# Input projections by seven block products, values first, with the recurrence done in place

## Chip, cores and metric

The kernel runs on one core of a Trainium2 chip. The metric is device time in microseconds, the median of the runs. The core has a matrix engine (TensorE, PE in the profile, with its weight loads as PEld), VectorE (DVE), ScalarE (ACT), GpSimd (POOL) and SyncE (SP), and queues of DMAs that SP and POOL feed.

## What is computed

A decoder trunk of two layers on 1024 tokens of width 1024. The change lies in the first layer's token mixer, a gated linear recurrence with 8 heads of 128:

```python
proj = h @ w_in                                   # (1024, 4 * 1024)
q, fz, v, g = jnp.split(proj, 4, axis=-1)
q = jax.nn.silu(q)
f = lb + (1 - lb) * jax.nn.sigmoid(fz)
k = 1 - f                                         # log_f = log(max(f, 1e-6))
# per head: S_t = diag(f_t) S_{t-1} + k_t v_t^T,  o_t = S_t^T q_t
o = o * rsqrt(mean(o * o over the head) + 1e-6) * norm_g
out = (o * jax.nn.silu(g)) @ w_out
```

After it come a normalisation with the residual and an MLP (squared ReLU, 4096 wide), then a second layer with a convolution module and an MLP. Those are the same in both kernels.

## The kernel before

**Numbers and products.** Every float32 operand is cut into a high part (ScalarE's copy to a narrower form) and a low part (VectorE's subtraction). A block product is three matmuls per block of the contraction: high by high, high by low, low by high (`product`, L303). Tokens are treated in two halves of 512. A wide matmul is one instruction of 128x512.

**Projections.** `x0T` holds the cut, transposed input, both halves. For each head, q and f (`narrow`, L326) are 8 contraction blocks by 3 matmuls for each half: 768 wide matmuls over all heads, called `ps<-x0T,wa`. Values (`values`, L588) and output gates (`gates`, L432) are computed by token blocks (`wide`, L330): 384 each. Together 1536. The weights come in through `Slots` (L57), which loads by SP, cuts, and keeps a few slots ahead.

**The MLPs already use seven products.** Both MLPs split their matrices into 2x2 blocks and use seven block products in place of eight (`ORDER`, L43: the forms 1, 2, 6, 5, 7, 3, 4); sums of the blocks are needed as operands. For the down weights those sums are made in DRAM by `block_sums` (L402): SP writes one word from a tile that must be ready first (L407), then issues two copies of 1 MB (L408, L409); POOL issues an accumulating DMA of 1 MB (L410) and two of 512 KB (L412), each waiting for the one before it. Fourteen such sums are issued by recurrences 0 to 11, two by each of the first two; the word comes from the recurrence's output tile `o`.

**Recurrence.** `recurrence` (L475) runs 16 times, for 8 heads and 2 halves; I number these 0 to 15. It builds decay products by doubling: at each level n, F and G hold running products from the left and from the right, and `qn`, `kn` (double-buffered) are q and k weighted for that level. Matmuls of `kn` by `qn` give blocks of the score matrix, which a predicated copy with a mask (`put`) brings into A. The levels are 4 (`kd`, `qd`, with reciprocals), 8, 16, 32, 64. Then k is transposed, A and the carried state are multiplied with the values, the state is stepped four times on VectorE, and `o` is stored to DRAM (L581, L582). The heads' norm and gate come later, in `gates`, after reading the heads back; there POOL does the power (L387) of a small tile `ss`.

**Order.** Python emits the work interleaved; a scheduler then fixes one order per engine, and every engine takes its own queue in that order. PSUM has eight banks; the recurrence uses banks 3 to 7 by name (`rps`). The output projection follows the last gates, then the first normalisation.

Of the kernel before, what the change touches and what calls it, by code (L numbers as in the profile page):

```python
# [15 lines left out]
P = 128  # L16
# [220 lines left out]
def body(ctx, tc, d, out):  # L237
# [103 lines left out]
    xraw, rraw = raws(run(128, 4, 4) + run(80, 4, 4)), raws(run(200, 5, 4))  # L341
    wa = Slots(nc, vector, slots(run(96, 4, 8), "wa"), rraw)
    x0T = [half_x(0, "x0T"), half_x(32, "x0T")]

    def load_x(h):
        xt = x0T[h]
        for k in range(0, KB, 2):
            raw = xraw().rearrange("p (a b) -> p a b", a=2)
            nc.sync.dma_start(out=raw, in_=d["xT"][h, :, k : k + 2, :])
            for i in range(2):  # L350
                nc.scalar.copy(out=xt[:, 0, k + i, :], in_=raw[:, i])  # L351
                vector.tensor_tensor(out=xt[:, 1, k + i, :], in0=raw[:, i], in1=xt[:, 0, k + i, :].bitcast(F32), op=ALU.subtract)
            yield xt

    for h in range(H):
        wa.plan([d["wqf"][h, 0], d["wqf"][h, 1]])

    wq, wf, x0 = wa.load(2), wa.load(2), load_x(0)
    for it in (wq, x0, wf, x0, wq, wf, x0, x0):
        next(it)  # L360
    wide_t, rows = (HT,), (NTB, P)
    wv = Slots(nc, vector, slots(run(160, 4, 8), "wv"), rraw)
    wv.plan([d["wv"][n, i] for n in range(2) for i in range(4)] + [d["wg"][0, i] for i in range(4)])
    wv.ahead(4)
    nc.sync.dma_start(out=par, in_=d["par"])
    for _ in load_x(1):
        pass
    vs = ring((64, 80), (2 * NTB, HT), "v")
    p2 = Room(((208, 212),), {"sg": (wide_t, 1), "sq2": (wide_t, 1)})
    p1 = Room(  # L370
        ((128, 160), (192, 200), (212, KBYTES)),
        {
            "mask": ((3, P), 1), "qn": (wide_t, 2), "kn": (wide_t, 2), "at": (rows, 2), "sq": (wide_t, 1), "q": (wide_t, 2), "k": (wide_t, 2),
            "F": (wide_t, 2), "G": (wide_t, 2), "qd": (wide_t, 2), "kd": (wide_t, 2), "dec": ((NTB,), 2), "kt": (rows, 2), "o": (rows, 1), "state": ((P,), 2),
        },
    )
    p1.rings.update(p2.rings)
    rraw = raws(run(200, 2, 4))
    wa.raws = wv.raws = rraw
# [3 lines left out]
    one = cst.tile([P, 1], F32, name="one")  # L383
    nc.gpsimd.memset(one, 1.0)
# [3 lines left out]


    lg = par[:, LB : LB + H]  # L390
    sm = cst.tile([P, 4, H], F32, name="sm")
    lb, oml = cst.tile([P, H], F32, name="lb"), cst.tile([P, H], F32, name="oml")
# [5 lines left out]
    vector.tensor_scalar(out=oml, in0=lb, scalar1=-1.0, scalar2=1.0, op0=ALU.mult, op1=ALU.add)  # L398

# [21 lines left out]


    od = [[dram.tile([P, NTB, HT], F32, name=f"od{n}{h}") for h in range(2)] for n in range(2)]
    yn = [[None, None], [None, None]]

    def heads_back(n):
        for half in range(2):
            yn[n][half] = view(64 + 16 * n + 8 * half, (NTB, HT), F32, "yn")
            nc.sync.dma_start(out=yn[n][half], in_=od[n][half])

    def gates(n, half, t, ws):

        if True:
            ps = acc()
            product(ps, wide(x0T[half], t, ws))
            ov = yn[n][half][:, t, :]
            sg = p2("sg")
            nc.scalar.activation(sg, ps, AF.Sigmoid)
            vector.tensor_tensor(out=sg, in0=ps, in1=sg, op=ALU.mult)
            sq = p2("sq2")  # L440
            nc.scalar.activation(sq, ov, AF.Square)
            ss = stat.tile([P, 2, 4], F32, tag="ss", name="ss")
            vector.tensor_reduce(out=ss[:, 0], in_=sq.rearrange("p (a b) -> p a b", a=4), op=ALU.add, axis=mybir.AxisListType.X)
            nc.gpsimd.tensor_scalar(out=ss[:, 1], in0=ss[:, 0], scalar1=1.0 / P, scalar2=RMS_EPS, op0=ALU.mult, op1=ALU.add)
            power_m_half(ss[:, 0], ss[:, 1], 4)
            for j in range(4):
                oj = ov[:, j * P : (j + 1) * P]
                vector.scalar_tensor_tensor(
                    out=oj, in0=oj, scalar=ss[:, 0, j : j + 1], in1=sg[:, j * P : (j + 1) * P], op0=ALU.mult, op1=ALU.mult
                )  # L450
# [6 lines left out]
    mask = p1("mask")  # L457
    nc.sync.dma_start(out=mask, in_=d["mask"])
    qn, kn, at = ([p1(n) for _ in range(2)] for n in ("qn", "kn", "at"))
    for t in qn + kn + at:  # L460
        nc.gpsimd.memset(t, 0.0)
    count = {"nk": 0, "at": 0}
    vts, carry = {}, {}

    def lr(t, n):
        v = t.rearrange("p (b h n) -> p b h n", h=2, n=n)
        return v[:, :, 0, :], v[:, :, 1, :]

    def last(v, n):
        return v[:, :, n - 1 : n].to_broadcast([P, v.shape[1], n])  # L470
# [4 lines left out]
    def recurrence(h, half, zq, zf, carry):  # L475
        sq = p1("sq")
        nc.scalar.activation(sq, zq, AF.Sigmoid)
        q = p1("q")
        vector.scalar_tensor_tensor(out=q, in0=zq, scalar=QSCALE, in1=sq, op0=ALU.mult, op1=ALU.mult)
        k = p1("k")  # L480
        nc.scalar.activation(k, zf, AF.Sigmoid)
        nc.scalar.activation(k, k, AF.Identity, bias=lb[:, h : h + 1], scale=oml[:, h : h + 1])
        yield
        vt, state = vts[h // 4][0], carry[h]
        F = p1("F")
        vector.tensor_scalar(out=F, in0=k, scalar1=GATE_EPS, scalar2=None, op0=ALU.max)
        nc.scalar.activation(k, k, AF.Identity, bias=one, scale=-1.0)

        G = p1("G")
        (f_l, f_r), (g_l, g_r) = lr(F, 1), lr(G, 1)  # L490
        nc.scalar.copy(out=g_l, in_=f_r)
        nc.vector.memset(g_r, 1.0)
        mul(f_r, f_r, f_l)
# [6 lines left out]
        double(2)  # L500

        (f_l, f_r), (g_l, g_r) = lr(F, 4), lr(G, 4)
        qd = p1("qd")
        kd = p1("kd")
        (q_l, q_r), (k_l, k_r) = lr(q, 4), lr(k, 4)
        vector.reciprocal(lr(qd, 4)[0], g_l)
        mul(lr(qd, 4)[0], q_l, lr(qd, 4)[0])
        mul(lr(qd, 4)[1], q_r, f_r)
        mul(lr(kd, 4)[0], k_l, g_l)
        vector.reciprocal(lr(kd, 4)[1], f_r)  # L510
        mul(lr(kd, 4)[1], k_r, lr(kd, 4)[1])
        A = at[count["at"] % 2]
        count["at"] += 1
        pd = ps1("pd")
        for c in range(NTB):
            tensor.matmul(pd[:, c, :], kd[:, c * P : (c + 1) * P], qd[:, c * P : (c + 1) * P], start=True, stop=True)
# [3 lines left out]

        put(0, pd)
        double(4)
        pc = None
        for n in (8, 16, 32, 64):
            i = count["nk"] % 2
            count["nk"] += 1
            mul(lr(qn[i], n)[1], lr(q, n)[1], lr(F, n)[1])
            mul(lr(kn[i], n)[0], lr(k, n)[0], lr(G, n)[0])
            if n == 8:
                pe = ps1("pe")  # L530
            elif n == 16:
                pc = ps1("pc")
            for c in range(NTB):
                if n <= 16:
                    tensor.matmul(
                        (pe if n == 8 else pc)[:, c, :], kn[i][:, c * P : (c + 1) * P], qn[i][:, c * P : (c + 1) * P], start=True, stop=True
                    )
                else:
                    for s in range(0, P, 2 * n):
                        tensor.matmul(  # L540
                            pc[s : s + n, c, s + n : s + 2 * n],
                            kn[i][:, c * P + s : c * P + s + n],
                            qn[i][:, c * P + s + n : c * P + s + 2 * n],
                            start=True,
                            stop=True,
                        )
            if n == 8:
                put(1, pe)
            double(n)
        put(2, pc)  # L550

        mul(q, q, F)
        mul(k[:, : (NTB - half) * P], k[:, : (NTB - half) * P], G[:, : (NTB - half) * P])
        dec = p1("dec")
        nc.scalar.copy(out=dec, in_=F.rearrange("p (c n) -> p c n", n=P)[:, :, P - 1])
        pk = ps1("pd")
        nk = NTB - half
        for c in range(nk):
            tensor.transpose(pk[:, c, :], k[:, c * P : (c + 1) * P], ident)
        kt = p1("kt")  # L560
        nc.scalar.copy(out=kt[:, :nk], in_=pk[:, :nk])
        po = ps1("po")
        for c in range(NTB):
# [754 lines left out]
```

## Time and profile before

| what | value |
|---|---|
| median of 3 runs | 2153.34 us (2152.73 to 2157.03) |
| span of the profiled execution | 2158.7 us; the page gives no other time for it |
| TensorE busy | 2132.6 us |
| VectorE, ScalarE, POOL busy | 1452.6, 959.1, 374.9 us |
| mean granted TensorE clock | 0.997 |
| first wide matmul | at 6.5 us |
| end of the output projection and its transposes | at 584.3 us |

The page lists groups of instructions by line, engine and operation: busy time, mean duration, and the idle time of that engine ahead of them with what ended it. Other views list waits, instructions in order of time, and busy time by stretches. Idle time on an engine that isn't the bound costs nothing. Helpers record many operations under one line (L172), so the names of tiles tell them apart.

### The profile page before, as it was taken

How to read it: one execution, taken by the hardware profiler on the slowest of the kernel's cores; microseconds unless marked ns; L12 is line 12 of the kernel's file. 1: busy time of each engine (PE TensorE's matmuls, PEld its weight loads, DVE VectorE, ACT ScalarE, POOL GpSimd, SP SyncE). 2: the span in 40 equal slices, each digit the busy share in tenths (PEclk: the TensorE clock that was granted, in tenths of full speed). 3: DMA queues.
4: the chain of work that ended last, by engine and by line, in shares of the span. 5: the costliest groups of instructions: out<-in, count | busy, mean ns of one | idle time of the engine just before them, and what ended most of it. 6: DMA issues, size and time to landing. Idle time of an engine off the chain costs nothing.

```text
span 2158.7 us, 27277 instructions
## 1 busy us (share of the span) xinstructions
PE 2132.6 (99%) x10248; PEld 1772.1 (82%) x10248; DVE 1452.6 (67%) x2107; ACT 959.1 (44%) x1349; POOL 374.9 (17%) x365
## 2 busy tenths in 40 slices
PE   8999999999999999999999999999999999999998
PEld 7888788888888888888888888888878888888887
DVE  7478799867777666556666798899627443554446
ACT  4222232232155555544444576567543443433333
POOL 0011121021100000000001599189211000000001
PEclk9999999999999999999999999999999999999999
DMA  4598888931247776899998855565595988865652
GB/s 182 154 235 227 199 236 214 228 128 59 79 128 272 276 252 227 291 382 322 347 328 313 304 185 186 205 244 174 172 314 189 335 318 310 307 201 194 195 164 99
DMA packets 161349, 494.99 MB, mean 229 GB/s; under 512 B 15040, under 2 KB 43968, under 8 KB 159680
## 3 DMA queue, kind: packets, MB, share of 16 engines
q1 hardware_dynamic: 152256, 459.69, 60.6%
q0 software_dynamic: 8960, 33.56, 8.8%
q8 instruction: 80, 1.31, 0.2%
q14 instruction: 53, 0.43, 0.1%
HBM read 370.50 MB, written 189.79 MB: 260 GB/s over the span
## 4 chain that ended last, share of the span: by engine, by line
PE 86%; DMA 7%; POOL 3%; DVE 2%; ACT 1%; issue 1%; SPq 0%; DVEq 0%; POOLq 0%
PE ps L172 86%; POOL cb L172 2%; DMA y<-kept 1%; DMA raw<-in_w_dram 1%; DMA wa<-ready 1%; DMA raw<-in_wv_dram 1%; DMA dh<-hf 1%; DMA raw<-in_wg_dram 1%; DVE wa L172 0%; DMA raw<-in_wqf_dram 0%; DVE y L172 0%; ACT prod L1086 0%; DMA raw<-in_xT_dram 0%; ACT wa L69 0%; ACT wv L69 0%
## 5 line engine op out<-in xcount | busy, mean ns | idle before, releaser
L172 PE MATMUL ps<-dw,dh 128*128 128x512 f32 x2688 | 611.2, 389 | 0.2 <-ACT dh L69 0.2
L172 PEld LDWEIGHTS ps<-dw,dh 128*128 128x128 f32 x2688 | 504.1, 188 | 104.9 <-ACT dh L69 0.6
L172 PE MATMUL ps<-x1f,fw 128*128 128x512 f32 x1344 | 307.9, 390 | 1.2 <-ACT fw L69 0.8
L172 PEld LDWEIGHTS ps<-x1f,fw 128*128 128x128 f32 x1344 | 251.4, 188 | 53.7 <-ACT fw L69 1.2
L172 PE MATMUL ps<-xa,wa 128*128 128x512 f32 x1152 | 268.8, 392 | 0.0
L172 PEld LDWEIGHTS ps<-xa,wa 128*128 128x128 f32 x1152 | 214.3, 188 | 43.5
L172 POOL TENSOR_TENSOR cb<-cb,prod 128x512 f32<-128x512 f32 x176 | 234.6, 1342 | 17.5 <-ACT prod L1086 7.0
L172 DVE TENSOR_TENSOR dh<-dh 128x1024 fp32r<-128x1024 f32 x112 | 136.3, 1222 | 117.4 <-ACT dh L69 117.2
L172 DVE TENSOR_TENSOR dw<-dr,dw 128x1024 fp32r<-128x1024 f32 x112 | 136.6, 1222 | 103.0 <-ACT dw L69 102.5
L172 DVE SCALAR_TENSOR_TENSOR ps<-u,par,ps 128x512 f32<-128x512 f32 x288 | 198.6, 749 | 9.9 <-ACT ps L1098 8.5
L172 PE MATMUL ps<-x0T,wa 128*128 128x512 f32 x768 | 190.6, 400 | 6.5 <-ACT x0T L351 6.5
L69 ACT CAST dh<-dh 128x1024 fp32r<-128x1024 f32 x112 | 117.0, 1051 | 149.2 <-DMA dh<-hf 148.9
L69 ACT CAST dw<-dr 128x1024 fp32r<-128x1024 f32 x112 | 117.4, 1053 | 134.1 <-PE ps L172 127.8
L172 PE MATMUL ps<-xc,wa 128*128 128x512 f32 x768 | 174.4, 389 | 0.0
L172 PEld LDWEIGHTS ps<-x0T,wa 128*128 128x128 f32 x768 | 143.7, 191 | 35.7 <-ACT x0T L351 6.5
L172 PEld LDWEIGHTS ps<-xc,wa 128*128 128x128 f32 x768 | 144.1, 188 | 29.8
L387 POOL TENSOR_TENSOR mv<-mv,nhalf 128x1 f32<-128x1 f32 x32 | 46.3, 1449 | 687.7 <-DVE mv L172 687.7
L69 ACT CAST wa<-raw 128x1024 fp32r<-128x1024 f32 (+1 forms) x77 | 79.0, 1028 | 192.8 <-PE ps L172 164.7
L172 DVE TENSOR_TENSOR wa<-raw,wa 128x1024 fp32r<-128x1024 f32 (+1 forms) x77 | 95.9, 1248 | 83.4 <-ACT wa L69 83.2
L1086 ACT ACTIVATE prod<-u,par 128x512 f32<-128x512 f32 x176 | 125.3, 722 | 54.4 <-POOL cb L172 53.7
L172 PE MATMUL ps<-wv,x0T 128*128 128x512 f32 x576 | 141.3, 395 | 1.1 <-DVE wv L172 0.8
L172 PEld LDWEIGHTS ps<-wv,x0T 128*128 128x128 f32 x576 | 106.1, 188 | 23.2 <-DVE wv L172 1.1
(177 smaller groups left out, 2606.9 us busy)
## 6 DMA issues: line engine op xcount, KB each, us to landing
wa<-ready SPq DMA_DIRECT2D x122, 512.0 KB, 5.0
dh<-hf SPq DMA_DIRECT2D x112, 512.0 KB, 4.4
ready<-spare SPq DMA_DIRECT2D x74, 512.0 KB, 4.6
sum_w<-in_w_dram SPq DMA_DIRECT2D x32, 1024.0 KB, 9.1
dr<-sum_w SPq DMA_DIRECT2D x64, 512.0 KB, 6.1
raw<-in_w_dram SPq DMA_DIRECT2D x51, 512.0 KB, 3.6
dr<-in_w_dram SPq DMA_DIRECT2D x48, 512.0 KB, 5.5
raw<-in_w1q_dram SPq DMA_DIRECT2D x36, 512.0 KB, 4.4
```

What stands on the lines that cost most here:

```text
L69: self.nc.scalar.copy(out=slot[:, 0, c], in_=raw[:, c])
L172: return op(*args, **kw)
L387: nc.gpsimd.tensor_tensor(out=dst, in0=src, in1=nhalf[:, :n], op=ALU.pow)
L1086: nc.scalar.activation(tp, u[:, k : k + HT], AF.Copy, scale=tap(j, k))
```

## The change

**Projections.** Input, values, q/f pairs and gate pairs are split into 2x2 blocks: two token halves, two halves of the contraction (or of the columns). Seven forms of the input (`XF`) are cut once and kept. Values come first: seven forms of their weights, four matmul groups each, results combined and written to DRAM (`vd`), from where each recurrence loads its 128 columns. Then come 12 pairs in the order `PAIRS`: one pair is either q and f of one head ("q") or the gates of two heads ("g"). Each pair is seven products of 12 wide matmuls. The block sums of a pair's weights are made by POOL (`pool_add`), one pair ahead; ring `fs` holds eight cut forms.

**Recurrence.** It is a generator with about twelve steps, and `advance` runs two or three steps between products. q and k of a recurrence lie in one tile `qk`. One table `T` holds the products of whole blocks at all levels; each level multiplies q's right halves and k's left halves in place by one merged product (`grow`), after the matmuls of that level have read them. The anchor level uses `rm` and one product `kd` on POOL over q and k together. The norm's sums come from ScalarE (`accum_out`), the power from POOL (L429), and ScalarE scales `o` by it; then `o` is transposed through the bank "pe", weighted and stored by heads (`od`). `block_sums` is still issued by the recurrence, with a word of the now normed `o`.

**Gates.** `gate_out` loads a stored head, multiplies it with its gate on POOL and stores it (`zd`); the last two heads skip that way. The output projection's operands are cut from there during the last pair.

```diff
+    def v_products(i):
+        for t, parts in enumerate(v_form(i)):
+            product(banks[:, 4 + t] if i in (2, 5, 3) else banks[:, t], parts, i in (1, 2, 5))
+            v_out(i, t)
...
+    def pair_forms(p):
+        b0, b1, b2, b3 = r0[:, :HT], r0[:, HT:], r1[:, :HT], r1[:, HT:]
+
+        def put(raw):
+            s = fs()
+            cut(s[:, 0], s[:, 1], raw)
+            made.append(s)
+
+        put(b0)
+        pool_add(rs7, b0, b2)
+        pool_add(b2, b2, b3)
+        yield
+        put(b1)
+        pool_add(b0, b2, b0)
+        yield
+        put(b0)
+        pool_add(b1, b0, b1)
+        yield
...
+        if p + 1 < len(PAIRS):
+            pair_load(p + 1)
+        yield
...
-    def recurrence(h, half, zq, zf, carry):
-        sq = p1("sq")
...
-        def double(n):
-            (f_l, f_r), (g_l, g_r) = lr(F, n), lr(G, n)
-            mul(g_l, g_l, last(f_r, n))
-            mul(f_r, f_r, last(f_l, n))
...
-            mul(lr(qn[i], n)[1], lr(q, n)[1], lr(F, n)[1])
-            mul(lr(kn[i], n)[0], lr(k, n)[0], lr(G, n)[0])
...
+    def recurrence(h, half):
+        B = qk[h, half]
+        Q, K = B[:, 0], B[:, 1]
+        vt = vts.pop(2 * h + half)
+        load_values(2 * h + half + 1)
...
+        def total(n):
+            t = totals[n].rearrange("p (b s) -> p s b", s=2)
+            mul(totals[2 * n], t[:, 0], t[:, 1])
+
+        def grow(n, k=True):
...
+            o = cutout(Q, n, [[HT - n, 2], [2 * n, nb], [1, n]])
+            mul(o, o, cutout(totals[n], 0, [[1, 2], [2, nb], [0, n]]))
...
+        vector.reciprocal(cutout(rm, 0, [[P + 1, 2], [2, P // 2]]), cutout(rt, 0, [[1, 2], [2, P // 2]]))
         kd = p1("kd")
...
+        pool.tensor_tensor(
+            out=kd.rearrange("p a (b n) -> p a b n", n=4), in0=B.rearrange("p a (b n) -> p a b n", n=4),
+            in1=cutout(rm, 0, [[P, 2], [1, P], [0, 4]]), op=ALU.mult,
+        )
+        total(4)
+        grow(4)
+        yield
...
+        yield state
+        ss = stat.tile([P, 2, 4], F32, tag="ss", name="ss")
+        sq = p1("sq")
+        for c in range(NTB):
+            nc.scalar.activation(sq[:, c * P : (c + 1) * P], po[:, c, :], AF.Square, scale=1.0 / QSCALE, accum_out=ss[:, 0, c : c + 1])
+        vector.tensor_scalar(out=ss[:, 1], in0=ss[:, 0], scalar1=1.0 / P, scalar2=RMS_EPS, op0=ALU.mult, op1=ALU.add)
+        power_m_half(ss[:, 0], ss[:, 1], 4)
         o = p1("o")
-        nc.scalar.activation(o, po, AF.Copy, scale=1.0 / QSCALE)
-        nc.sync.dma_start(out=od[h // 4][half][:, :, h % 4 * P : (h % 4 + 1) * P], in_=o)
+        for c in range(NTB):
+            nc.scalar.activation(o[:, c], po[:, c, :], AF.Copy, scale=ss[:, 0, c : c + 1])
         for _ in range(2 if 2 * h + half < 2 else 1 if 2 * h + half < 12 else 0):
             block_sums(*to_sum.pop(0), o[:2, 0, :1])
...
+        pt = ps1("pe")
+        for c in range(NTB):
+            tensor.transpose(pt[:, c, :], o[:, c], ident)
+        on = p1("u" if h == H - 1 else "on")
+        nc.scalar.activation(on, pt.rearrange("p a b -> p (a b)"), AF.Copy, scale=nrm[:, h : h + 1])
...
+    def gate_out(h, half):
+        u = p1("u")
+        nc.sync.dma_start(out=u, in_=od[h][half])
+        g = gates.pop((h, half))
+        pool.tensor_tensor(out=u, in0=u, in1=g, op=ALU.mult)
+        nc.sync.dma_start(out=zd[half][:, h, :], in_=u)
...
+        for i in ORDER:
+            if kind == "q" and i == 2:
+                while recs and recs[0][0] <= j - 2:
+                    advance()
+            pair_product(p, i, made.pop(0), st)
+            if forms:
+                next(forms)
+            rate += (24 if p in (1, len(PAIRS) - 1) else 16) / 7
+            while rate >= 1:
+                rate = rate - 1 if advance() else 0.0
+            gate_some()
...
```

More of the change, by code (lines that the diff above doesn't have):

```diff
@@ L340, in body @@
     ident = cst.tile([P, P], F32, name="ident")
[L341 to L353, printed above, removed]
@@ L378, in body, with cut @@
-    rraw = raws(run(200, 2, 4))
-    wa.raws = wv.raws = rraw
+    wide_t, rows = (HT,), (NTB, P)
+    XF, VS, VO = {}, {}, {}
+    x00, x10, x01, x11, t6 = [view(kb, (4, HT), F32, "xr") for kb in run(112, 5, 8)]
+    a0, a1, a2, a3, s7 = [view(kb, (2, 1024), F32, "vr") for kb in run(152, 5, 8)]
+    vd = [[dram.tile([P, NTB, HT], F32, name=f"vd{m}{n}") for n in range(2)] for m in range(2)]
+    def cut(hi, lo, raw):
+        nc.scalar.copy(out=hi, in_=raw)
+        vector.tensor_tensor(out=lo, in0=raw, in1=hi.bitcast(F32), op=ALU.subtract)
@@ L419, in form @@
         return {1: w[0], 2: w[1], 6: t[2], 5: t[1], 7: t[0], 3: t[3], 4: w[3]}[i]
[L423 to L450, printed above, removed]
@@ L455, in ps1 @@
         return banks[:, 7, :P] if name == "pst" else banks[:, rps[name]].rearrange("p (a b) -> p a b", a=NTB)
[L457 to L470, printed above, removed]
+    count = {"at": 0}
@@ new lines, in body, with advance @@
+    recs, done = [], set()
+    def advance():
+        nonlocal carry
+        if not recs:
+            return False
+        h, half, gen = recs[0]
+        if gen is None:
+            gen = recs[0][2] = recurrence(h, half)
+        try:
+            got = next(gen)
+            if got is not None:
+                carry = got
+        except StopIteration:
+            recs.pop(0)
+            done.add((h, half))
+        return True
+    def gate_out(h, half):
[4 more added lines that the diff above has]
+        nc.sync.dma_start(out=zd[half][:, h, :], in_=u)
@@ new lines, in gate_some @@
+    def gate_some(force=False):
+        for h, half in sorted(gates):
+            if h >= H - 2:
+                continue
+            while force and (h, half) not in done:
+                advance()
+            if (h, half) in done:
+                gate_out(h, half)
+    oT, back = [], []
+    wb_at, wa_at, wb_raw, wa_raw = iter((136, 144, 152, 128)), iter((112, 120, 96, 104)), [], []
+    wb = Slots(nc, vector, lambda: view(next(wb_at), (2, 1024), F32R, "wb"), lambda: wb_raw[0]())
+    wa = Slots(nc, vector, lambda: view(next(wa_at), (2, 1024), F32R, "wa"), lambda: wa_raw[0]())
@@ new lines, in last_head @@
+    def last_head(half):
+        while (H - 1, half) not in done:
+            advance()
+        u, g = lastly[half], gates.pop((H - 1, half))
+        mul(u, u, g)
+        into(half, H - 1, u)
+    pair_load(0)
+    forms = pair_forms(0)
+    for _ in range(4):
+        next(forms)
+    v_products(3)
+    cut_v(4, a3)
+    v_products(4)
+    fs.views += [view(kb, (2, HT), F32R, "fs") for kb in run(136, 4, 4)]
+    p1 = Room(
+        ((160, KBYTES),),
+        {
+            "qk": ((2, HT), 4), "kd": ((2, HT), 1), "t": (wide_t, 4), "sq": (wide_t, 2), "at": (rows, 2), "f": (wide_t, 2), "T": (wide_t, 2),
+            "kt": (rows, 1), "o": (rows, 2), "on": (wide_t, 1), "u": (wide_t, 2), "mask": ((3, P), 1), "rm": ((2, P), 1), "state": ((P,), 2),
+        },
+    )
```

433 lines of the change are left out of this document (290 added, 143 removed).

## The prediction

> **What bounds the kernel now.** I read the page first, then the busy time by stretches, then the waits. The page's head, its busy line and its chain:
>
> ```profile
> span 2158.7 us, 27277 instructions
> PE 2132.6 (99%) x10248; PEld 1772.1 (82%) x10248; DVE 1452.6 (67%) x2107; ACT 959.1 (44%) x1349; POOL 374.9 (17%) x365
> PE 86%; DMA 7%; POOL 3%; DVE 2%; ACT 1%; issue 1%; SPq 0%; DVEq 0%; POOLq 0%
> ```
>
> TensorE is busy 99% of the span and holds 86% of the chain that ends last; GpSimd (POOL) is busy 17%. The change touches only what lies before the first MLP, so the stage that matters runs from the first matmul to the end of the output projection. Its row in the view of stretches (busy time of each engine, then clock, DMA share, GB/s):
>
> ```profile
> 6.00:584.00 578.00, 569.34 (x3213) 478.37 (x3214) 436.11 (x868) 162.44 (x265) 75.51 (x87) 0.99 0.66 178
> ```
>
> TensorE works 569 of 578 us. So a matmul less is a gain, as long as TensorE's queue still never waits. What will matter is hidden by POOL's 75 us of work; the waits from 0 to 560 us show the other side of it:
>
> ```profile
> POOL sum_w L410 <- DMA sum_w<-in_w_dram: 146.7, 10, 68.5
> POOL sum_w L412 <- DMA sum_w<-in_w_dram: 102.5, 12, 11.7
> POOL sum_w L412 <- DMA sum_w<-sum_w: 78.1, 14, 11.1
> ```
>
> POOL stands for 327 us (68.5 of them ahead of the first) in front of the DMAs with which `block_sums` adds blocks of the down weights in DRAM. Now that costs nothing: almost nobody needs POOL in this stage.
>
> **The change part by part.** *Removed from TensorE.* The four projections go from 8 block products to 7:
>
> ```profile
> L172 PE MATMUL ps<-x0T,wa 128*128 128x512 f32 x768 | 190.6, 400 | 6.5 <-ACT x0T L351 6.5
> ...
> L172 PE MATMUL ps<-wv,x0T 128*128 128x512 f32 x576 | 141.3, 395 | 1.1 <-DVE wv L172 0.8 <-ACT wv L69 0.3
> ```
> ```profile
> 554.54 5.61 PE L172 MATMUL ps<-wa,x0T 128*128 128x512 f32 x24
> 559.99 1.03 PE L172 MATMUL ps<-ident,t 128*128 128x128 f32 x8
> ```
>
> 768 + 576 + 192 (the second gate half) = 1536 matmuls become 1344; 24 of them took 559.99 - 554.54 = 5.45 us, 0.227 each. 192 x 0.227 = **43.6 us less**: 569 - 44 = 526 us of TensorE work. The 16 recurrences keep their small matmuls: 569 less 1920 x 0.227 (projections and output) and about 14 for transposes is 119, or 7.4 us each. The head transposes move, same count.
>
> *Added beside TensorE.* VectorE works 436 us of the 578; per level of the recurrence one merged product and a short table entry replace four products, and the cuts and block sums of the projections come back for that. ScalarE stays near a third. Values and gated heads take a turn through DRAM (4 + 4 and 3 + 3 MB, 1 less for the heads' own), some 13 MB more at a DMA share of 0.66. These I cost at nothing: TensorE's 526 us cover them. If that cover failed for DMA, 13 MB at the stage's 178 GB/s would be 73 us.
>
> *Moved to POOL.* Adds for weight forms, gate products, the anchor product `kd` and the power of the norm:
>
> ```profile
> L172 POOL TENSOR_TENSOR cb<-cb,prod 128x512 f32<-128x512 f32 x176 | 234.6, 1342 | 17.5 <-ACT prod L1086 7.0
> ```
> ```profile
> L387 POOL TENSOR_TENSOR ss<-ss,nhalf 128x4 f32<-128x4 f32 x16 | 16.4, 1029 | 1.2
> ```
>
> So 1.34 us for an add of 128x512, 2.7 for `kd` (twice as wide), 1.03 for a power: about 190 us in all, little for an engine that has the whole stage. But they join the queue that stands before DMAs, and that queue runs in order. VectorE's sums and then POOL, before the change:
>
> ```profile
> 288.36 0.69 DVE L172 TENSOR_REDUCE ss<-sq 128x4 f32<-128x512 f32 x1 [1.24 <-ACT sq L441]
> ...
> 320.75 0.67 DVE L172 TENSOR_REDUCE ss<-sq 128x4 f32<-128x512 f32 x1
> ```
> ```profile
> 294.08 0.82 POOL L412 DMA_DIRECT2D sum_w<-sum_w  x1 [6.71 <-DMA sum_w<-sum_w]
> 294.99 0.19 POOL L444 TENSOR_SCALAR ss<-ss 128x4 f32<-128x4 f32 x1
> ...
> 327.97 1.17 POOL L410 DMA_DIRECT2D sum_w<-in_w_dram  x1 [9.64 <-DMA sum_w<-in_w_dram]
> 329.22 0.19 POOL L444 TENSOR_SCALAR ss<-ss 128x4 f32<-128x4 f32 x1
> ```
>
> A sum ready at 289.05 is taken up at 294.99, one ready at 321.4 at 329.22, each time just behind a DMA issue that had waited. In the changed kernel's order on POOL, the power of recurrence r+1 stands behind all three POOL DMAs of recurrence r, for r = 1 to 11. Those DMAs read `o` of r, and `o` needs the power of r. That closes **a loop**: power(r), `o`(r), two copies on SP, three accumulating DMAs on POOL one after the other, power(r+1). TensorE waits in it, because the transposes of `o` stand in its fixed order, and the next recurrence's first blocks use the same bank.
>
> Its length, from `o` to the last of the three issues, in two recurrences of before:
>
> ```profile
> 228.04 0.58 ACT L581 ACTIVATE o<-ps 128x512 f32<-128x512 f32 x1
> ...
> 346.91 0.60 ACT L581 ACTIVATE o<-ps 128x512 f32<-128x512 f32 x1
> ```
> ```profile
> 242.30 1.17 POOL L410 DMA_DIRECT2D sum_w<-in_w_dram  x1 [8.19 <-DMA sum_w<-in_w_dram]
> 254.24 0.88 POOL L412 DMA_DIRECT2D sum_w<-sum_w  x1 [10.77 <-DMA sum_w<-in_w_dram]
> 261.53 0.82 POOL L412 DMA_DIRECT2D sum_w<-sum_w  x1 [6.41 <-DMA sum_w<-sum_w]
> ...
> 357.24 1.26 POOL L410 DMA_DIRECT2D sum_w<-in_w_dram  x1 [10.06 <-DMA sum_w<-in_w_dram]
> 365.92 0.87 POOL L412 DMA_DIRECT2D sum_w<-sum_w  x1 [7.41 <-DMA sum_w<-in_w_dram]
> 373.14 0.80 POOL L412 DMA_DIRECT2D sum_w<-sum_w  x1 [6.35 <-DMA sum_w<-sum_w]
> ```
>
> 261.5 - 228.6 = 32.9 us, and 373.1 - 347.5 = 25.6. I take 28, nearer the shorter, since the loop will space these DMAs further apart. To it come the last issue 0.8, the power 1.0 and the first part of `o`, about 0.3: 30.1 per recurrence. What stands on POOL between the last issue and the power adds 18 adds and 6 `kd` over the nine steps from recurrence 3 to 12: 24 + 16 = 40 us. Nine steps: 9 x 30.1 + 40 = 311. Recurrences 0 and 1 issue two sums each:
>
> ```profile
> 72.51 0.60 ACT L581 ACTIVATE o<-ps 128x512 f32<-128x512 f32 x1 [2.12 <-PE ps L172]
> ```
> ```profile
> 82.22 1.34 POOL L410 DMA_DIRECT2D sum_w<-in_w_dram  x1 [68.46 <-DMA sum_w<-in_w_dram]
> 98.44 1.16 POOL L410 DMA_DIRECT2D sum_w<-in_w_dram  x1 [14.88 <-issue]
> 99.14 1.33 POOL L412 DMA_DIRECT2D sum_w<-sum_w  x1
> ...
> 115.66 0.84 POOL L412 DMA_DIRECT2D sum_w<-sum_w  x1 [3.19 <-DMA sum_w<-sum_w]
> ```
>
> From `o` to the first L412 26 us (then power 1: with what is in between 33), and laid out the same way 38 and 34 for the next two: 105. The loop lasts 105 + 311 = **416 us**, from `o` of recurrence 0 to `o` of 12 (12 to 15 issue no sums).
>
> *TensorE in that time.* Its order has 660 wide matmuls and one recurrence ahead of the loop (157 us) and 423, three recurrences and transposes after it (96 + 22 + 7 = 125). In between lie 526 - 157 - 125 = 244 us. So it idles 416 - 244 = 172. At the end, recurrences 13 to 15 run with few matmuls between their steps, 16 us uncovered by my count; the start, in smaller loads, 6 more.
>
> The stage then ends at 6 + 526 + 172 + 16 + 6 = 726 in place of 584: **+142 us**. The trace gives the profiled execution's span alone, 2158.7, 5 us over the median; 142 on the median 2153.3 is 2295.
>
> *The clock.* Where TensorE waited before:
>
> ```profile
> 246.30:250.30 4.00, 0.03 (x1) 0.92 1.04 220
> ...
> 252.00:254.00 2.00, 2.00 (x11) 0.50 0.71 252
> ...
> 256.00:258.00 2.00, 2.00 (x9) 0.88 0.93 127
> ```
>
> After 4 us of waiting the granted clock was 0.50 for some 6 us, a loss of 3. Twelve waits of the loop will each bring that; inside the loop it is taken from the idle time, and in the tail it is part of the 16. The Trainium skill (TensorE: Matmul & The Clock Gate, What's actually happening) has half clock after an idle window of about 3.4 us, and full clock again after a busy window of that length. By that the loss would be 1.7 per wait, not 3; the sum does not move.
>
> **The rivals.** *The loop is short and the in-place recurrence sets the pace.* The rows for the DMAs themselves, to landing:
>
> ```profile
> sum_w<-in_w_dram POOLq DMA_DIRECT2D x14, 1024.0 KB, 10.3
> sum_w<-sum_w POOLq DMA_DIRECT2D x28, 512.0 KB, 7.3
> ```
>
> Were they to land 10 us sooner in all once the queue is emptier, the loop's nine steps would take 220 and it would no longer decide. Then this does:
>
> ```profile
> L172 DVE COPY_PREDICATED at<-mask,ps 128x512 f32<-128x512 int32 x48 | 35.2, 734 | 16.7 <-PE ps L172 16.0
> ...
> L172 DVE TENSOR_TENSOR q<-q,F 128x512 f32<-128x512 f32 x16 | 10.9, 682 | 0.0
> ```
>
> Each level's product (0.68) overwrites what the level's matmuls (0.9, four at a time) have just read, so VectorE and TensorE take turns over five levels: 8 us, with two mask copies, four state steps and the norm about 17 us per recurrence, 7 of them TensorE's. TensorE's order leaves some 25 us of this uncovered per four recurrences: 75 for three such rounds. The stage ends at 6 + 526 + 75 + 16 + 6 = 629, +45: 2198. The Trainium skill (DMA: Bandwidth & Descriptors, Anatomy of one DMA — SWDGE (gpsimd) path) fits 2.0 us plus bytes over 436e3 for such a DMA, 4.4 and 3.2 us here as an estimate; by it this rival would hold. The rows above, 10.3 and 7.3, disagree.
>
> *Faster: both chains stay covered.* Place: POOL's queue. If the loop closes within TensorE's own 244/12 = 20 us per recurrence, that is with 14 us from `o` to the last issue, and the turns hide behind projections, only start and tail are lost: 6 + 526 + 16 + 6 = 554, -30: 2123. For it: 526 us of work is really gone from 569. Against it: no recurrence of before did it in under 25.6.
>
> *A longer loop.* With 33 us (the 228.04 row) and SP's queue late, since stores of gated heads wait there for POOL ahead of the copies: +45 and +20 make 2360.
>
> **How the numbers follow.** The loop as counted 0.76, with the longer loop in it, own range 2235 to 2365; in-place turns 0.14 (2198); covered 0.08 (2123); near no change 0.02. The range for 8 in 10 reaches from the turns to past the longer loop: 2175 to 2385. A measurement of this kernel can tell about 0.2% from no change: faster 0.08, same 0.02, slower 0.90.
>
> **What would show it.** POOL: `sum_w` waits followed at once by the power or an add, and ScalarE's `o` waiting for POOL. TensorE: idle some 170 us more between about 170 and 590, in a dozen waits of over 4 us, clock 0.5 behind each; `o` spaced 30 to 42 us. It is wrong if the powers run well ahead of the accumulating DMAs, if `o` comes every 20 us, or if TensorE waits mostly for VectorE's `qk` with POOL long done. The 1344 matmuls at 0.227 should show in any case.

## The result and the profile after

The changed kernel takes 2361.6 us (median of 4 runs, 2359.8 to 2366.1) against 2154.9 (2152.7 to 2157.0): 1.096 times, 95% interval 1.094 to 1.098. That is 207 us slower; the prediction had said 142 slower. The page of the changed kernel, its head, busy line and chain:

```profile
span 2358.0 us, 27326 instructions
PE 2169.4 (92%) x10056; PEld 1787.7 (76%) x10056; DVE 1466.4 (62%) x1938; ACT 1040.2 (44%) x1607; POOL 547.6 (23%) x458
PE 68%; DMA 15%; DVE 6%; POOL 5%; issue 3%; ACT 2%; SPq 0%; DVEq 0%; POOLq 0%
```

TensorE executes 192 instructions less (10056 for 10248), as planned, and yet is busy 37 us longer; its share of the chain falls from 86% to 68%. The first matmul of the first MLP shows where the stage ends, and the view of stretches what happened in it:

```profile
783.84 6.61 PE L172 MATMUL ps<-x1f,fw 128*128 128x512 f32 x28
```
```profile
6.00:783.80 777.80, 606.22 (x3023) 493.84 (x3022) 449.71 (x702) 240.82 (x522) 247.21 (x179) 0.86 0.55 149
```

The stage ends at 783.8 in place of 584.3, 199.5 us later. What follows it lasts 2358.0 - 783.8 = 1574.2, and lasted 2158.7 - 584.3 = 1574.4 before. So the whole loss lies in this stage. There TensorE idles 777.8 - 606.2 = 172 us (9 before), and it is busy 606 us with work that the prediction counted as 526 at full clock: its mean granted clock is 0.86, not 0.99. Busy time times what the granted clock lacks, summed over stretches of 2 us, is 70 us here; the other 10 are not explained. So 172 + 80 = 252 us are lost, where the prediction had 194. Who ended the waits (first 800 us), for TensorE, then for POOL and VectorE:

```profile
PE ps L172 <- ACT o L683: 51.1, 8, 16.8
PE ps L172 <- DVE qk L172: 50.0, 44, 5.1
```
```profile
POOL sum_w L498 <- DMA sum_w<-in_w_dram: 80.0, 11, 11.5
...
POOL sum_w L496 <- DMA sum_w<-in_w_dram: 51.2, 8, 8.5
POOL sum_w L498 <- DMA sum_w<-sum_w: 45.5, 12, 5.7
```
```profile
DVE qk L172 <- POOL kd L172: 35.7, 7, 12.7
```

Eight long waits for `o` and 44 short ones for VectorE's level products weigh the same. The loop of the prediction is there, and one turn of it reads so, in order of time (only the rows of the loop):

```profile
406.61 0.81 POOL L498 DMA_DIRECT2D sum_w<-sum_w  x1 [3.56 <-DMA sum_w<-sum_w]
...
407.17 2.27 POOL L172 TENSOR_TENSOR kd<-qk,rm 128x1024 f32<-128x1024 f32 x1
...
409.48 0.69 DVE L172 TENSOR_TENSOR qk<-qk,T 128x512 f32<-128x512 f32 x1 [2.58 <-POOL kd L172]
...
411.36 1.03 POOL L429 TENSOR_TENSOR ss<-ss,nhalf 128x4 f32<-128x4 f32 x1 [1.91 <-DVE ss L172]
...
412.42 1.14 ACT L683 ACTIVATE o<-ps,ss 128x128 f32<-128x128 f32 x4 [3.13 <-POOL ss L429]
...
412.84 1.25 PE L172 MATMUL ps<-ident,o 128*128 128x128 f32 x4 [5.17 <-ACT o L683]
```

POOL issues the last accumulating DMA after standing before it, then at once `kd`, which belongs to the recurrence after; VectorE had waited for that `kd`, and behind it in VectorE's queue stands the rest of the recurrence whose norm is due. The power runs 4 us later and waits for VectorE. So in this turn the loop closes at `kd`, one step ahead of the power on which the prediction had built. Four turns read so (last issue at 289.7, 406.6, 436.5 and 585.3 us). In others POOL itself waits for TensorE before `kd` (8.6 us at 377, 9.2 us at 519), and no DMA holds the recurrence up there. But is the loop the cause of 200 us? The answer of the runs is: of a good quarter of it, in the order that this kernel has.

### The profile page after: what moved, and what is told of

It is laid out like the page before. It is cut to its first block, busy times and chain, and to the rows that moved or that the text cites. A ratio compares the mean times of both kernels' runs of the same rounds, so it can differ in the third digit from the quotient of the medians.

```text
span 2358.0 us, 27326 instructions
## 1 busy us (share of the span) xinstructions
PE 2169.4 (92%) x10056; PEld 1787.7 (76%) x10056; DVE 1466.4 (62%) x1938; ACT 1040.2 (44%) x1607; POOL 547.6 (23%) x458
## 4 chain that ended last, share of the span: by engine, by line
PE 68%; DMA 15%; DVE 6%; POOL 5%; issue 3%; ACT 2%; SPq 0%; DVEq 0%; POOLq 0%
PE ps L172 68%; DMA sum_w<-in_w_dram 4%; DMA raw<-in_wqf_dram 3%; POOL cb L172 2%; DVE qk L172 2%; DMA raw<-in_w_dram 1%; DMA sum_w<-sum_w 1%; DMA y<-kept 1%; DMA wa<-ready 1%; DVE fs L172 1%; DMA vr<-in_wv_dram 1%; DMA dh<-hf 1%; POOL ss L429 1%; DMA raw<-in_wg_dram 1%; POOL kd L172 1%
## 5 line engine op out<-in xcount | busy, mean ns | idle before, releaser
L172 PE MATMUL ps<-xf,fs 128*128 128x512 f32 x1008 | 269.5, 427 | 21.2 <-ACT t L736 19.5
L172 PEld LDWEIGHTS ps<-xf,fs 128*128 128x128 f32 x1008 | 205.7, 208 | 69.8 <-ACT t L736 21.1
L429 POOL TENSOR_TENSOR mv<-mv,nhalf 128x1 f32<-128x1 f32 x32 | 47.4, 1483 | 655.5 <-DVE mv L172 655.5
L1190 POOL COPY next<-ss 128x1 f32<-128x1 f32 x37 | 15.9, 429 | 488.5 <-DVE spare L172 235.1
L172 DVE TENSOR_TENSOR qk<-qk,T 128x512 f32<-128x512 f32 x96 | 73.0, 762 | 89.4 <-PE ps L172 53.4
L349 ACT CAST fs<-raw 128x512 fp32r<-128x512 f32 x72 | 44.0, 619 | 173.6 <-POOL raw L172 67.5
L172 DVE TENSOR_TENSOR fs<-raw,fs 128x512 fp32r<-128x512 f32 x72 | 64.6, 902 | 87.5 <-ACT fs L349 86.9
```

The costliest lines, as they stand in the source:

```text
L172: return op(*args, **kw)
L349: nc.scalar.copy(out=hi, in_=raw)
L429: nc.gpsimd.tensor_tensor(out=dst, in0=src, in1=nhalf[:, :n], op=ALU.pow)
L1190: nc.gpsimd.tensor_copy(out=raw[:, :1], in_=now)
```

## Experiments

Twelve kernels ran, most once beside the kernel before on the same chip; times of one chip are compared by their ratio where a few us matter.

**Without the sums.**

```diff
-            block_sums(*to_sum.pop(0), o[:2, 0, :1])
+            to_sum.pop(0)                 # form() then takes plain blocks
```

> The changed kernel with the 14 block sums of the recurrences left out (plain blocks of the down weights stand in for them; copies and accumulating DMAs are gone, the rest is as it is). Loop theory (GpSimd stands before the accumulating DMAs, and work of the recurrence stands behind it on its queue): the stage up to the first matmul of the first MLP, which ends at 784 us with the sums, ends between 555 and 630 us, so 2130 to 2205 us in all. Turn-taking theory (VectorE and TensorE alternate over the levels in place, whatever GpSimd does): the waits of TensorE for VectorE stay and with them most of the time, over 2290 us.

Measured: 2302.7 us, only 59 less. The loop theory falls as the main cause: POOL is free, and 148 us of the loss are still there. The stage and TensorE's waits in this run:

```profile
6.00:725.90 719.90, 599.69 (x3022) 487.13 (x3022) 441.22 (x702) 241.27 (x521) 206.32 (x137) 0.89 0.24 79
```
```profile
PE ps L172 <- DVE qk L172: 36.1, 34, 3.3
PE ps L172 <- ACT o L684: 25.1, 10, 2.9
...
PE ps L172 <- DVE state L172: 13.8, 27, 2.2
```

The stage ends at 725.9: 120 us idle and 74 of busy time over 526, at a clock of 0.89 (61 of the 74 by the clock, counted as above). No wait for a recurrence's step is longer than 3.3 us. Two recurrences of this run on TensorE, in order of time, show what those waits are:

```profile
353.42 1.05 PE L172 MATMUL ps<-qk 128*128 128x128 f32 x8
355.93 1.16 PE L172 MATMUL ps<-qk 128*128 128x128 f32 x8 [1.47 <-DVE qk L172]
358.96 0.45 PE L172 MATMUL ps<-qk 128*32 128x32 f32 x16 [1.87 <-DVE qk L172]
360.27 0.82 PE L172 MATMUL ps<-qk 128*64 128x64 f32 x8 [0.86 <-DVE qk L172]
...
372.03 1.25 PE L172 MATMUL ps<-ident,o 128*128 128x128 f32 x4 [2.71 <-ACT o L684]
```
```profile
406.81 5.74 PE L172 MATMUL ps<-xf,fs 128*128 128x512 f32 x24 [1.92 <-ACT t L737]
412.47 0.45 PE L172 MATMUL ps<-qk 128*32 128x32 f32 x16
412.85 5.28 PE L172 MATMUL ps<-xf,fs 128*128 128x512 f32 x22
418.06 0.68 PE L172 MATMUL ps<-qk 128*64 128x64 f32 x8
418.67 6.19 PE L172 MATMUL ps<-xf,fs 128*128 128x512 f32 x26
```

From 353.6 to 373 not one projection matmul stands between the steps of a recurrence, and each level waits about a microsecond or two for VectorE. Fifty microseconds later two steps are covered by 72 projection matmuls (24, 22 and 26), 17 us of work beside a chain that needs two or three. The cover is there, but TensorE's queue has it in the wrong places.

**The kernel before without the sums** (the same edit).

> The kernel before with the same 14 block sums left out. If GpSimd's 327 us of standing before those DMAs cost nothing there, the time stays within 6 us of 2154. If they hold the stage up there as well, it gets faster by more than 10 us.

Measured: 2149.0, 5.9 less, in one run each: about nothing, as the prediction said of the kernel before.

**Plain copies in place of the accumulating DMAs, first try.**

```diff
-        nc.gpsimd.dma_start(out=v[:, 0:2], in_=w[:, 2:4], accum_op=ALU.add)
-        for i in (2, 3):
-            nc.gpsimd.dma_start(out=v[:, i], in_=v[:, i - 1], accum_op=ALU.add, max_dma_last_dim=4096)
+        nc.sync.dma_start(out=e[:, 0:2], in_=w[:, 2:4])
+        for i in (2, 3):
+            nc.sync.dma_start(out=e[:, i], in_=w[:, i - 1])
```

> The changed kernel with each of the 42 accumulating DMAs of GpSimd in the recurrences replaced by a plain copy of the same size on SyncE's queue into memory that nobody reads (the sums themselves are so left out). Loop theory: traffic is not the cause, so within 20 us of the run without sums. Contention theory (the added traffic slows loads and with them the stage): it stays above 2290 us, near the changed kernel.

Measured: 2357.9, and it tells nothing of the traffic in the loop: having nothing to wait for, the copies were laid ahead of everything and began at 20 us.

```profile
20.46 0.69 SPq L500 DMA_DIRECT2D else_w<-in_w_dram  x1
```
```profile
PE ps L172 <- ACT xf L349: 40.4, 1, 40.4
```

TensorE stood once for 40 us before a form of the input (`xf`), whose loads go through the same queue. **Paced copies**, where a word written from `o` comes ahead of them (and the two 512 KB copies are one of 1 MB), repair that:

> The changed kernel (its own order) with each recurrence's three accumulating DMAs of GpSimd replaced by two plain copies of the same 2 MB on SyncE's queue into memory that nobody reads, each behind a word written from o, so that they start where the sums did (the sums are left out). GpSimd's queue then holds no DMA. If the sums' 59 us (2362 against 2303 without them) come from GpSimd standing before the accumulating DMAs: 2295 to 2320 us. If they come from the traffic or from SyncE's queue: 2335 to 2365 us.

Measured: 2311.2, or 1.069 of the kernel before beside it, as the run without sums (2302.7 of 2154.9, 1.069). With the traffic kept (159 GB/s over a stage of 727.3 us, 149 over 777.8 with the sums: 116 MB each) and no DMA in POOL's queue, nearly all of the 59 us are gone: they are the price of POOL standing before accumulating DMAs. That an accumulating DMA may load the memory in another way than a plain copy of its size is not separated from this.

**The power off POOL's queue, then power and `kd`.**

```diff
-        power_m_half(ss[:, 0], ss[:, 1], 4)
+        nc.vector.reciprocal(ss[:, 0], ss[:, 1])
```
```diff
-        pool.tensor_tensor(
+        vector.tensor_tensor(
             out=kd.rearrange("p a (b n) -> p a b n", n=4), in0=B.rearrange("p a (b n) -> p a b n", n=4),
```

The second kernel has both edits, the first one only the upper. Both leave out the root of the norm.

> The changed kernel with the norm's power of the recurrences taken off GpSimd's queue: VectorE computes a reciprocal in its place (the root is left out). Sums, kd, adds and gate products stay on GpSimd. Theory of the prediction (the power behind the last accumulating DMA closes the loop): most of the loss goes, 2180 to 2240 us. Theory from the profile after (kd stands first behind the last accumulating DMA and VectorE's levels wait for kd, so the loop closes one step earlier): little goes, 2320 to 2360 us.

> The changed kernel with the sums in place, but kd and the norm's power (as a reciprocal, the root left out) on VectorE: only adds of weight forms, swish and gate products are left behind the accumulating DMAs on GpSimd. The sums cost 59 us in the changed kernel (2362 against 2303 without them). If they cost it by GpSimd's queue through kd and the power: 2295 to 2325 us. If by the adds and gate products that stay there, or by DMA traffic: 2340 to 2365 us.

Measured: 2353.0 with the power alone (9 us less), 2342.4 with both (1.084 of the kernel before beside it in place of 1.096, some 26 us less). The 9 us are hardly more than single runs differ by; the power alone was not the link. Nor are power and `kd` together all of it. Weight adds, swish and gate products still stand behind the DMAs, and by elimination they take the rest; no run moved them alone. The trace of the second kernel fits: ScalarE waits 36.8 us for POOL's gate products `u` there and 53.0 us for its weight adds `raw`, against 22.8 and 38.5 without the sums. What costs is the queue, not one operation in it.

**Filler matmuls in the run without sums.** Is the half clock a cause? In the run without sums the clock falls to half behind bare recurrences. Behind one of them:

```profile
300.00:302.00 2.00, 0.65 (x6) 0.46 (x5) 1.70 (x3) 0.26 (x1) 0.05 (x1) 1.00 0.00 0
302.00:304.00 2.00, 1.22 (x4) 0.93 (x4) 0.69 (x3) 0.49 (x4) 0.00 (x0) 0.66 0.00 0
304.00:306.00 2.00, 0.00 (x0) 0.00 (x0) 0.61 (x3) 1.30 (x8) 1.07 (x2) 0.50 0.25 68
...
312.00:314.00 2.00, 2.00 (x12) 1.72 (x11) 0.49 (x1) 0.62 (x1) 0.00 (x0) 0.78 0.40 123
```

```diff
+    def warm(n=2):
+        for _ in range(0 if oT else n):
+            nc.tensor.matmul(banks[:, 7, P:], XF[1][:, 0, 0, :P], XF[1][:, 0, 1, : HT - P], start=True, stop=True)
```

> The run without sums, with 24 filler matmuls of 384 columns added per recurrence (two ahead of each level and each state step, six ahead of the transposes of o) for all recurrences up to the last few: at 0.17 us each some 4 us per recurrence, 55 us in all, into a part of a bank that nobody reads. In the run without sums TensorE is idle 120 us in the stage and its granted clock there is 0.89, with stretches at 0.50 behind each recurrence. Clock theory (the half clock follows stretches in which TensorE works little, and some 70 us of the loss are matmuls at half clock): the clock of the stage rises above 0.94 and the time falls below 2290 us although work is added. Other theory (the clock follows something else, or the waits alone count): the clock stays near 0.89 and the time is 2300 to 2360 us.

Measured: 2305.9, 1.067 of the kernel before beside it (1.069 without fillers).

```profile
L575 PE MATMUL ps<-xf 128*128 128x384 f32 x360 | 80.4, 357 | 15.3 <-DVE state L172 15.2
```
```profile
6.00:730.60 724.60, 636.04 (x3382) 534.05 (x3381) 447.37 (x702) 241.77 (x522) 206.13 (x137) 0.94 0.23 79
```

The clock rose from 0.89 to 0.94, as the clock theory had it; the time did not fall, as it had not. 360 fillers of 384 columns, 0.227 x 384/512 = 0.17 us each, are 61 us of work at full clock (80.4 busy as they ran). But the run does not show that they cost nothing, nor that the clock is no cause. The queue as laid put most of them elsewhere than the source: 18 of a recurrence's 24 stand in one piece ahead of the transposes of `o`, and none between the levels, which still run at half clock when they are bare. Twelve projection matmuls behind recurrence 4, first without and then with fillers, and the way of recurrence 6 from a level to its transposes with them (355.93 to 372.03 without):

```profile
308.37 5.10 PE L172 MATMUL ps<-xf,fs 128*128 128x512 f32 x12 [0.72 <-ACT t L737]
```
```profile
316.70 3.06 PE L172 MATMUL ps<-xf,fs 128*128 128x512 f32 x12 [0.41 <-ACT t L746]
...
362.22 1.16 PE L172 MATMUL ps<-qk 128*128 128x128 f32 x8 [1.42 <-DVE qk L172]
...
381.52 0.60 PE L172 MATMUL ps<-ident,o 128*128 128x128 f32 x4
```

The twelve gain 2.0 us by the clock; the bare way takes 19.3 us where it took 16.1. So it goes on: from `o` of recurrence 0 to `o` of 15, the six turns that took over 32 us without fillers shrink by 19 us together, and the nine others grow by 17. A higher clock does gain time where projection matmuls stand, and the fillers lose about as much where the chain of a recurrence, from engine to engine, sets the pace. The half clock is a second price of the bare stretches, paid in the matmuls behind them; what it would be worth alone no run shows.

**The recurrence in place, alone.** The levels of the changed kernel put into the kernel before, whose projections, norm and order stay:

```diff
-            mul(lr(qn[i], n)[1], lr(q, n)[1], lr(F, n)[1])
-            mul(lr(kn[i], n)[0], lr(k, n)[0], lr(G, n)[0])
...
-            double(n)
+            o = cutout(Q, n, [[HT - n, 2], [2 * n, nb], [1, n]])
+            mul(o, o, cutout(totals[n], 0, [[1, 2], [2, nb], [0, n]]))
```

> The kernel before with the recurrence's levels of the changed kernel alone (products in place, one merged decay product per level, kd on GpSimd); projections, norm, gates, sums and order as before. Theory of the cover (the recurrence in place is no slower where enough projection matmuls stand between its steps; what hurts is that the changed kernel leaves it little cover): within 20 us of 2154. Theory of the turns (products in place make VectorE and TensorE alternate wherever they stand): over 2200 us. Theory of the GpSimd queue (kd behind accumulating DMAs): over 2200 us here and near 2154 with kd on VectorE.

> As the kernel before with the recurrence in place, but kd computed by VectorE, so that nothing of the levels stands on GpSimd's queue. Theory of the cover: within 20 us of 2154. Theory of the turns: over 2200 us. The difference to the run with kd on GpSimd is the price of GpSimd's queue there: over 15 us if that queue decides, under 5 us if not.

Measured: 2209.6 with `kd` on POOL and 2161.9 with `kd` on VectorE, beside 2161.0 before. With POOL out of it, products in place and one merged product per level cost nothing and gain nothing in that order of work. The one operation on POOL costs 48 us:

```profile
DVE qk L172 <- POOL kd L172: 83.0, 9, 15.8
```
```profile
PE ps L172 <- DVE qk L172: 33.7, 7, 8.2
```

VectorE waits nine times for `kd` (the first row, VectorE's waits; 15.8 us the longest), TensorE seven times for the level products behind it. Here a short operation behind POOL's waits stands alone, and its price is shown in a kernel in which the same sums cost nothing before. It is `kd` and not the power, so it bears out the prediction's queue, not its link.

**Another order of issue.** One word in the last lines lets the framework lay the same instructions out without its simulated timeline:

```diff
-    with tile.TileContext(nc, schedule_with_timeline_sim=True) as tc, ExitStack() as ctx:
+    with tile.TileContext(nc, schedule_with_timeline_sim=False) as tc, ExitStack() as ctx:
```

The third of the kernels with it also issues the sums later, one DMA at every second weight form (`tick`):

```diff
-            block_sums(*to_sum.pop(0), o[:2, 0, :1])
...
             up.form(c, i, f)
+            tick(f[:2, 1, :1].bitcast(F32))       # and the same per form in down_all
```

> The changed kernel with one word changed in its last lines: the framework lays the engines' queues without its simulated timeline (False for True). The same instructions; in TensorE's queue the steps of a recurrence then stand one by one between groups of 1 to 12 projection matmuls, where they stood in bunches of up to 25 instructions with some 108 projection matmuls in one piece behind four recurrences. Theory of the order (the chain of a recurrence is bare because TensorE's queue has bunched it): 40 to 150 us faster than 2362, though the sums still stand on GpSimd's queue. Theory of the chain alone (a recurrence takes 25 us or more however it is mixed, and 16 of them follow each other): within 40 us of 2362.

> Control: the kernel before with the same word changed. If the order as such gains or loses in the whole kernel, it shows here: within 30 us of 2155 expected, since TensorE is busy 99% of the time either way; a loss of more than 30 us would mean that the other stages suffer from the other order, and that the runs of the changed kernel with it have to be read by the stage alone.

> The changed kernel with that other order, and with its 14 block sums issued later: one DMA of GpSimd per two weight forms in the first MLP's up and down projections, each behind the landing of the one before; nothing is left out. If sums and order are the two causes and add up: the stage ends between 550 and 640 us and the time is 2125 to 2215 us, near the kernel before and perhaps ahead of it. If the later sums cost as much in the MLP as in the recurrences: 40 us or more above that. If the order is no cause: 2300 us or more.

Measured in all: 2414.0, 2272.9 (the control) and 2476.0 (1.144, interval 1.142 to 1.147). No time came where its expectation had put it; the third kernel's stage end did. The control says that this order harms the other stages by itself: the kernel before loses 110 us with it, but its first stage ends only 8 us later, at 592.7. So these runs are read by that stage. With the sums in place it ends at 735.8, with the sums out of it at 631.9:

```profile
735.82 4.38 PE L172 MATMUL ps<-x1f,fw 128*128 128x512 f32 x18
```
```profile
6.00:632.00 626.00, 553.76 (x3024) 440.40 (x3024) 466.29 (x703) 237.86 (x523) 211.37 (x137) 0.97 0.27 91
```

In that second kernel TensorE idles 72 us and its clock is 0.97. Its queue in a recurrence:

```profile
355.59 0.60 PE L172 MATMUL ps<-ident,qk 128*128 128x128 f32 x4
356.03 0.61 PE L172 MATMUL ps<-v,at 128*128 128x128 f32 x4
356.39 0.94 PE L172 MATMUL ps<-xf,fs 128*128 128x512 f32 x3
357.21 0.49 PE L172 MATMUL ps<-v,kt 128*128 128x128 f32 x2
```

Three projection matmuls stand between two steps, and no row has a wait. With the sums in place, the first of the two kernels waits like this (first 736 us), and in its clearest turns POOL reads as in the second view:

```profile
PE ps L172 <- ACT o L683: 76.7, 15, 13.5
```
```profile
362.52 0.81 POOL L498 DMA_DIRECT2D sum_w<-sum_w  x1 [4.92 <-DMA sum_w<-sum_w]
363.07 1.33 POOL L429 TENSOR_TENSOR ss<-ss,nhalf 128x4 f32<-128x4 f32 x1
```

Fifteen waits for `o` are half of TensorE's 156 us of idle time there. In five turns the power runs at once behind an accumulating DMA, as in this view; in most others POOL's adds and products come between. So in this order the loop that the prediction described is the largest single cause. The times of the stage's end make a table:

| | sums in the recurrences | without them there | difference |
|---|---|---|---|
| order with the simulated timeline | 783.8 | 725.9 | 57.9 |
| other order | 735.8 | 631.9 | 103.9 |
| difference | 48.0 | 94.0 | |

Sums and order together are 152 of the 199.5 us. ("Without them there" is, in the other order, the kernel that issues them in the MLP.) The 47.6 left (631.9 - 584.3) are 43.6 us of work saved, against 63 more of idle time (72 - 9) and 28 more of busy time (554 - 526), of which the clock explains 14, counted as above. The late sums were no way out, though: behind the stage that kernel lasts 2476.5 - 631.9 = 1844.6 us, where the first one, in the same order, lasts 2411.8 - 735.8 = 1676.0. They cost the MLP 169 us, more than they had cost the recurrences. No run of the changed kernel beats the kernel before.

## Why the prediction was right, and where it was not

Direction, range and rough size were right; the weights inside were not.

- *1536 to 1344 matmuls, 43.6 us less*: the count is right, 10056 for 10248. How much of the gain arrived no run shows; in bare stretches the chain of a recurrence, and not TensorE's work, sets the pace.
- *Costs at nothing*: right for the sums of work. VectorE's 450 us in the stage (436 before) and ScalarE's 241 are no bound, and the recurrence in place, alone, is 2161.9 against 2161.0. The added traffic is there as counted (149 GB/s x 777.8 us less 178 x 578 is 13 MB); none of TensorE's waits in the stage is put down to a DMA, but no run priced it alone. Not at nothing are VectorE's products as links of a bare chain: 44 waits, 50.0 us.
- *The loop over POOL*: there, but mis-sized. Forecast: 172 us of TensorE's idle time, and with it nearly all of +142. TensorE idled 137.5 of the 437.6 us from 187.6 to 625.2, but leaving the sums out gains only 58 us as the kernel is, 104 in the other order. Two reasons. The time without the loop was set too low, since removing it uncovers the next chain. And the link was not the power alone (9 us) but POOL's whole queue, with `kd` worth more than the power.
- *Its length*: `o` of recurrences 0, 5 and 12 is scaled so:

```profile
187.61 1.14 ACT L683 ACTIVATE o<-ps,ss 128x128 f32<-128x128 f32 x4 [0.51 <-POOL ss L429]
...
382.61 1.14 ACT L683 ACTIVATE o<-ps,ss 128x128 f32<-128x128 f32 x4 [1.21 <-POOL ss L429]
626.48 1.13 ACT L683 ACTIVATE o<-ps,ss 128x128 f32<-128x128 f32 x4
```

  From `o` to the last issue 406.6 - 383.8 = 23 us in this turn, where 28 was taken. Yet the whole lasts 626.5 - 187.6 = 439 us for a forecast of 416, 37 us per recurrence: a turn is not only the DMAs but also what is left of the recurrence behind `kd`.
- *First and last parts*: `o` of recurrence 0 was put at 169 us and came at 187.6, and from `o` of 12 to the end it took 157 us for 141. With the 23 of the loop these are the 58 us by which the forecast of the stage's end, 726, was short.
- *The step that failed*: the time without the loop. "TensorE's order leaves some 25 us of this uncovered per four recurrences". In the run without sums `o` is scaled from 188 us (recurrence 0) to 657 (15):

```profile
L684 ACT ACTIVATE o<-ps,ss x64: 358/367/409, 188.0 to 657.5; 128x128 f32<-128x128 f32 x64
```

  That is 31 us for each, 125 per four; TensorE's work for four is three pairs (252 x 0.227 = 57) and 4 x 7.4, 87 us. So 38 are lost per four, idle or by the clock, where 25 were counted, and outside those rounds TensorE loses more too: 120 + 74 us in all, where that rival had 75 + 22. The working of the prediction counts TensorE's matmuls ahead of the loop, in it and after it, but not how they lie between the steps; the queue as laid does not spread them, and that is worth 94 us without the sums. The rival's mechanism, turns that TensorE's work does not cover, was there. That its 629 comes so near the 631.9 of the other order is largely chance: TensorE idles 24.9 us there before 187, 46.2 from 187 to 560 and 1.2 after, where the rival had 6 at the start, 75 and 16 at the end. That the run without sums ends the stage at 725.9, just where the forecast had put it with them, is chance: another mechanism fills the same size.
- *The clock*: that its loss inside the loop "is taken from the idle time" no run shows; the fillers ran without the loop, and there the clock did cost time behind bare stretches. Its size was too small, 3 us in each of twelve waits against 70 us in the stage, and a clock of 0.50 comes behind stretches with no long wait at all.
- *The rival "a longer loop"*: its 2360 is the time that was measured, 2361.6, and that is luck. Its condition, 33 us from `o` to the last issue, was not met: recurrences 3 to 11 took 22.5 to 26.4.
- *The rival "faster"*: its conditions, a loop within 20 us and turns hidden, were not met in any run of the changed kernel.

What stays open: how far each of the two orders is from the best one for this stage, and a place for the sums that costs neither the recurrences nor the MLP. Both were not tried further. That a mix of the two orders would give 631.9 + 1574 us is only arithmetic.

## What to carry to other kernels

When work leaves the engine that bounds a stage, ask first what that work was covering: a serial chain over several engines needs its cover spread between its steps, in the queue as it is laid, so read the order of the queue and not that of the program. A test that adds work to raise the clock moves two things at once; compare the stretches, not only the total. An operation moved to a queue that stands before DMAs inherits those waits, however short it is; count everything behind the wait, and not the one operation that looks critical. Before a price is put on one cause, work out the time with that cause taken away; here it was 148 us above the old time, not below it.

## What the hardware showed beyond that

- The half clock needs no long wait. In the 300 to 304 us rows above TensorE is busy 1.9 of 4 us, in pieces, and the granted clock is 0.66 and then 0.50 until past 312, some 10 us; before the change a wait of 4 us had led to 6 us of it. No gap in TensorE's work there is over 2.5 us, and none ahead of the drop over 2.1. The Trainium skill (TensorE: Matmul & The Clock Gate, What's actually happening) has a monitor of recent activity set the clock, over free-running windows of about 3.4 us; these rows agree with a measure of activity and not of one gap. How little activity is too little no run here shows.
- The time of an accumulating DMA moves with what is around it. From issue to landing the 512 KB ones took 7.3 us in the stage before, 5.6 in the changed kernel and 8.3 with the sums moved to the MLP; the 1 MB ones 10.3, 10.4 and 13.0. What causes the differences was not tested.
